# A hybrid decoder layer: the input projection as paired blocks with seven products, ahead of the three head groups

## The chip, the core and the metric

The kernel runs on one core of a Trainium2 chip. It is one program of five instruction streams, each in order: TensorE (PE; its weight loads are listed as PEld), VectorE (DVE), ScalarE (ACT), GpSimd (POOL) and SyncE (SP, which here only issues transfers). The metric is the device time of one launch in microseconds (us); the lower the better. The profile is one execution, taken by the hardware profiler.

## The reference

`x` has 1024 tokens of 1024 channels. All arithmetic is float32. One normalised input is projected onto 6144 channels, which feed three groups of heads:

```python
hn = rmsnorm(x, g_norm)
proj = hn @ w_in                      # [1024, 1024] @ [1024, 6144]
xm, zm, om, qa, ka, va, za, qx, zx = split(proj)   # 1024 x3, 512 x6
# mLSTM, 4 heads x 256
xc  = silu(causal_depthwise_conv(xm))
q_m, k_m, v_m = block_diag_proj(xc), block_diag_proj(xc), block_diag_proj(xm)
h_m = sigmoid(om) * mlstm_chunkwise(q_m, k_m / 16, v_m, *gates(q_m, k_m, v_m))
y_m = (head_layernorm(h_m) + skip * xc) * silu(zm)
# dilated attention, 8 heads x 64, three (window, dilation) patterns
y_a = dilated_attention(rope(qa), rope(ka), va) * silu(za)
# cross attention into 256 memory tokens, 4 heads x 128
kx, vx = split(rmsnorm(mem, g_mem) @ w_mem_kv)
y_x = softmax(qx @ kx.T / sqrt(128)) @ vx * silu(zx)
out = rmsnorm(x + concat(y_m, y_a, y_x) @ w_out, g_final)
```

## The kernel before

Every float32 operand of a large product is split in two parts of lower precision, `hi` and `lo`: ACT copies `hi`, DVE or POOL subtracts (`split`, L80–82). A product is then three matmuls: hi·hi, hi·lo, lo·hi. So TensorE's work is three times the plain one, and each operand costs one ACT and one DVE or POOL instruction.

The normalised input lies in SBUF for most of the run, transposed and split (`hnh`, `hnl`, eight buffers `hn` of 128 x 2 x 1024). Its weights come from DRAM in a stream of blocks, 36 channel blocks and 6 token blocks. A channel block (`ch_block`) computes 128 channels of all tokens in two halves of 512 tokens, with `proj_ch` (L161–169): 8 k-slices x 3 matmuls of 512 columns for each half. A token block (`t_block`) computes 256 channels with tokens on the partitions, in matmuls of 256 columns (L211–213). Each block has a `done` function that takes the result from PSUM: a gate `silu2` (L247–251), the rotation `rope` of queries and keys (L381–393, whose sine part needs four small transfers that swap rows), the convolution of the mLSTM (`xm_block`, L563–612), and so on. `wload` brings a block's weights, one block ahead, and splits them; a list `LO_ON_POOL` names the blocks whose `lo` POOL makes. Output blocks (`out_block`, `proj_t`, L177–179, result added by DVE at L853) stand in the same stream behind them.

The order of the work is written out in the program. The cross attention's units (head, half) come first, then the dilated attention's sixteen units, then the gates (`gates`) and the mLSTM's eight units (`head_weights`, `head_values`, `head_out`). Between the steps of a unit, `fill(n)` puts n pieces of the stream on TensorE:

```python
    for n, u in enumerate(units):
        a = head_weights(u)
        fill(HEAD_FILLS[n][0])
        if p2 is not None:
            head_out(units[n - 1], p2)
        fill(HEAD_FILLS[n][1])
        p2 = head_values(u, a)
```

So projections of x run beside the cross and the dilated attention, and output products beside the heads. On top of that a scheduler, which estimates when each operand is there, sets the final order of each engine's instructions. Results that wait for later stages (mLSTM gates `om`, `zm`, values `v`) go through DRAM; queries, keys, values and gates of the two attentions stay in SBUF, in the 13 buffers `g` of 128 x 1024. Temporaries of 128 x 512 share the four buffers `t2k`. PSUM has eight banks: `pj` 2, `s1` 3 (listed as `s`), `tp` 2, `po` 1.

## Time and profile before

| | before |
|---|---|
| timed runs, median (of 1070.48, 1071.22, 3581.81) | 1071.22 us |
| profiled execution, span | 1062.8 us |
| PE busy | 1030.0 us, 6528 matmuls |
| DVE, ACT, POOL busy | 700.4, 446.3, 309.8 us |
| moved by DMA | 117.03 MB, mean 110 GB/s |

A group's row in the profile names line, engine, operation, `output<-inputs` (buffer numbers left out), shape and count; then busy us, mean ns of one, and the engine's idle time ahead of it with what ended it. A row of busy time by stretch has the stretch, its length, busy us and instructions of each engine, the granted TensorE clock, the share of the DMA engines and GB/s. A row in order of time has start, duration, engine, line and operation; one of the chain that ended last has start, time on the chain, and what held it. A row of one line's instructions has count and shortest, median and longest duration in ns. A row of waits has the total in us, how many, and the longest.

### The profile page before, as it was taken

The page shows a single profiled execution, that of the slowest core. Times are in us where ns is not written, and L with a number is a line of the kernel's source. Part 1 is how long each engine was busy: PE and PEld are TensorE (multiplying, and loading weights), DVE is VectorE, ACT ScalarE, POOL GpSimd, SP SyncE. Part 2 cuts the span into 40 slices and gives each one's busy share as a digit, 9 for nine tenths or more (in the row PEclk, how much of TensorE's full clock was granted, in tenths as well). Part 3 has the DMA queues.
Part 4 walks back from the last instruction along what each step waited for, and adds up shares of the span by engine and source line. Part 5 has one row for each costly group of instructions (what it writes and reads, how often), then busy time and mean ns, then how long its engine had stood idle before and what let it go on. Part 6 is the DMA issues. An engine that isn't in the chain of part 4 may idle for free.

```text
span 1062.8 us, 17259 instructions
## 1 busy us (share of the span) xinstructions
PE 1030.0 (97%) x6528; PEld 920.1 (87%) x6528; DVE 700.4 (66%) x1458; ACT 446.3 (42%) x876; POOL 309.8 (29%) x296
## 2 busy tenths in 40 slices
PE   6899999999999999999999999989999999999996
PEld 4788888898889888778888888889999999999996
DVE  7865554545778578784748787735477877775375
ACT  5134433324556356563424444544344344331221
POOL 6531021408621263631000022211034144121352
PEclk8899999999999999999999999999999999999999
DMA  8333232314301131122214345344368454433332
GB/s 284 86 124 110 83 103 62 93 65 92 80 21 41 46 95 34 47 70 70 90 50 110 120 124 154 107 143 140 119 212 295 132 171 166 128 120 120 96 117 86
DMA packets 76435, 117.03 MB, mean 110 GB/s; under 512 B 14780, under 2 KB 46012, under 8 KB 76352
## 3 DMA queue, kind: packets, MB, share of 16 engines
q1 hardware_dynamic: 68032, 101.70, 29.7%
q0 software_dynamic: 8320, 14.23, 5.2%
q8 instruction: 51, 0.84, 0.3%
q14 instruction: 32, 0.26, 0.1%
HBM read 79.09 MB, written 31.57 MB: 104 GB/s over the span
## 4 chain that ended last, share of the span: by engine, by line
PE 78%; DVE 10%; DMA 6%; ACT 2%; issue 1%; POOL 1%; SPq 0%; POOLq 0%; DVEq 0%; ACTq 0%
PE pj L167 10%; PE pj L168 10%; PE pj L169 10%; PE pj L178 5%; PE pj L179 5%; PE pj L177 5%; PE pj L211 3%; PE pj L213 3%; PE pj L212 3%; PE tp L479 3%; DVE t2k L581 2%; DMA v<-P 2%; DMA wr<-in_w_out_dram 2%; PE s L454 2%; PE po L488 1%
## 5 line engine op out<-in xcount | busy, mean ns | idle before, releaser
L167 PE MATMUL pj<-hn,wh 128*128 128x512 f32 x544 | 216.8, 398 | 2.4 <-DVE t2k L249 1.3
L169 PE MATMUL pj<-hn,wl 128*128 128x512 f32 x544 | 217.0, 399 | 0.0
L168 PE MATMUL pj<-hn,wh 128*128 128x512 f32 x544 | 216.3, 398 | 0.0
L167 PEld LDWEIGHTS pj<-hn,wh 128*128 128x128 f32 x544 | 102.3, 188 | 25.6 <-DVE t2k L249 1.8
L81 ACT ACTIVATE wh<-wr 128x1024 fp32r<-128x1024 f32 x67 | 70.9, 1058 | 127.2 <-PE pj L168 53.8
L169 PEld LDWEIGHTS pj<-hn,wl 128*128 128x128 f32 x544 | 102.3, 188 | 22.7
L168 PEld LDWEIGHTS pj<-hn,wh 128*128 128x128 f32 x544 | 102.3, 188 | 22.3
L211 PE MATMUL pj<-wh,hn 128*128 128x256 f32 x384 | 107.9, 281 | 1.3 <-ACT st L262 1.3
L213 PE MATMUL pj<-wh,hn 128*128 128x256 f32 x384 | 107.5, 280 | 0.0
L212 PE MATMUL pj<-wl,hn 128*128 128x256 f32 x384 | 107.2, 279 | 0.0
L82 POOL TENSOR_TENSOR wl<-wr,wh 128x1024 fp32r<-128x1024 f32 x23 | 55.7, 2420 | 145.8 <-ACT wh L81 112.8
L82 DVE TENSOR_TENSOR wl<-wr,wh 128x1024 fp32r<-128x1024 f32 x44 | 57.0, 1296 | 46.5 <-ACT wh L81 34.9
L81 ACT ACTIVATE pth<-tp 128x512 fp32r<-128x512 f32 (+2 forms) x96 | 50.1, 540 | 73.3 <-PE tp L479 42.7
L82 DVE TENSOR_TENSOR ptl<-tp,pth 128x512 fp32r<-128x512 f32 (+2 forms) x96 | 58.0, 618 | 28.5 <-ACT pth L81 28.2
L211 PEld LDWEIGHTS pj<-wh,hn 128*128 128x128 f32 x384 | 72.1, 188 | 2.1 <-ACT st L262 1.5
L212 PEld LDWEIGHTS pj<-wl,hn 128*128 128x128 f32 x384 | 72.1, 188 | 0.4
L213 PEld LDWEIGHTS pj<-wh,hn 128*128 128x128 f32 x384 | 72.1, 188 | 0.2
L177 PE MATMUL pj<-wh,hn 128*128 128x256 f32 x256 | 71.9, 281 | 0.0
L178 PE MATMUL pj<-wl,hn 128*128 128x256 f32 x256 | 71.8, 280 | 0.0
L179 PE MATMUL pj<-wh,hn 128*128 128x256 f32 x256 | 71.7, 280 | 0.0
L462 ACT ACTIVATE P<-P,mx 128x128 f32<-128x128 f32 (+3 forms) x64 | 49.3, 772 | 21.1 <-DVE mx L458 20.8
L468 POOL TENSOR_SCALAR P<-P,ls 128x128 f32<-128x128 f32 (+4 forms) x40 | 29.2, 736 | 89.4 <-DVE ls L463 60.1
(323 smaller groups left out, 2682.4 us busy)
## 6 DMA issues: line engine op xcount, KB each, us to landing
wr<-in_w_all_dram SPq DMA_DIRECT2D x54, 512.0 KB
x<-v POOLq DMA_DIRECT2D x16, 516.0 KB, 4.5
wr<-in_w_out_dram SPq DMA_DIRECT2D x16, 512.0 KB
wr<-y SPq DMA_DIRECT2D x16, 512.0 KB
y<-t2k SPq DMA_DIRECT2D x24, 256.0 KB
v<-P SPq DMA_DIRECT2D x24, 256.0 KB
zm<-st SPq DMA_DIRECT2D x16, 256.0 KB
g<-g POOLq DMA_DIRECT2D x32, 128.0 KB, 2.7
```

The source lines that it names most:

```text
L81: S.activation(hi, src, AF.Copy)
L82: (eng_lo or V).tensor_tensor(lo, src, hi.bitcast(F32), op=SUB)
L167: PE.matmul(o, hi[:, ks], ah(k, cs), start=k == 0, stop=False)
L168: PE.matmul(o, hi[:, ks], al(k, cs), start=False, stop=False)
L169: PE.matmul(o, lo[:, ks], ah(k, cs), start=False, stop=k == KC - 1)
L177: PE.matmul(o, ah(k, cs), hi[:, ks], start=k == 0, stop=False)
L178: PE.matmul(o, ah(k, cs), lo[:, ks], start=False, stop=False)
L179: PE.matmul(o, al(k, cs), hi[:, ks], start=False, stop=k == nk - 1)
L211: PE.matmul(oi, hn_h(4 * kh + k, cs), hi[:, ks], start=kh == 0 and k == 0 and i == 0, stop=False)
L212: PE.matmul(oi, hn_h(4 * kh + k, cs), lo[:, ks], start=False, stop=False)
L213: PE.matmul(oi, hn_l(4 * kh + k, cs), hi[:, ks], start=False, stop=kh == 1 and k == 3 and i == 1)
L462: S.activation(pr, pr, AF.Exp, bias=mx, scale=-1.0, accum_out=ls)
```

## The change

The blocks of x that the start does not compute, 34 channel blocks and 6 token blocks, become 20 pairs, each computed in seven products of half the contraction length where plain block multiplication has eight. For two blocks and the two halves of the contraction, weights are `a11, a12` (first block, first and second half) and `a21, a22`; the input's quarters are `x11 .. x22` (halves of channels and of tokens). POOL makes three or four sums of weights for a pair (`unit_sums`, `unit_split`), the start makes four sums of the input (`t_build`), and DVE recombines the products from PSUM (`plus`, five additions for a pair of channel blocks, ten for a pair of token blocks).

All pairs come directly behind the start, as one stage, and all their results go to DRAM: queries with their split, rotated queries and keys, values, gates and the convolved channels `xc`. The convolution and the rotation are cut into steps in a queue `later`, of which one or two are taken behind each product. Then the mLSTM's eight units alternate with the eight of the cross attention, with only the memory's keys and values as projections. Then comes the dilated attention, whose operands `att_load` brings back from DRAM, with output products as filler, and at the end the output of that group. All weight and output splits of the stream put their `lo` on POOL. The sums of squares of x, and of the memory, are taken on TensorE by one-column matmuls against ones.

```diff
+    def t_build(k, xa, xb, t4s):
...
+        d, e = t2k(), t2k()
+        G.tensor_tensor(d, x12, x11, op=SUB)
+        G.tensor_scalar(e, x12, ga, None, op0=MUL)
+        t3, t2 = t2k(), t2k()
+        V.scalar_tensor_tensor(t3, x22, gb, e, op0=MUL, op1=SUB)
+        V.scalar_tensor_tensor(t2, x11, ga, t3, op0=MUL, op1=ADD)
...
+    def rope_done(dst, scale):
+        def done(half, o, in_sbuf):
...
+            c = t2k()
+            G.tensor_tensor(c, f, tabs["cos"][:, hs], op=MUL)
+
+            def turn():
+                G.tensor_tensor(f, sw, tabs["sin"][:, hs], op=MUL)
+                V.tensor_tensor(f, c, f, op=ADD)
+                hi, lo = st2(F32R), c.bitcast(F32R)
+                S.activation(hi, f, AF.Copy, scale=scale)
+                V.scalar_tensor_tensor(lo, f, scale, hi.bitcast(F32), op0=MUL, op1=SUB)
+                nc.sync.dma_start(dst[0][:, hs], hi.bitcast(F32))
+                nc.sync.dma_start(dst[1][:, hs], c)
+            later.append(turn)
...
+    def unit_sums(u):
...
+        G.tensor_tensor(s1_, a21, a22, op=ADD)
+        G.tensor_tensor(s2_, s1_, a11, op=SUB)
+        G.tensor_tensor(a21, a11, a21, op=SUB)
...
+    def unit_split(u, p):
+        a = sums[u][p]
+        if p == 3:
+            G.tensor_tensor(a, sums[u][2], sums[u][6], op=SUB)
...
+            split(t[:, :512], t[:, 512:], a)
...
+    def product(u, p, o, first, sub):
+        t, b = wps[u, p], side(p)
+        if units[u][0] == "c":
+            for k in range(4):
+                hi, lo = t[:, k * P:(k + 1) * P], t[:, 512 + k * P:512 + (k + 1) * P]
+                PE.matmul(o, hi, b(0, k), start=first and k == 0, stop=False, skip_group_check=True)
+                PE.matmul(o, hi, b(1, k), start=False, stop=False, skip_group_check=True)
+                PE.matmul(o, lo, b(0, k), start=False, stop=k == 3, skip_group_check=True)
...
+        if p == 1:
+            m["a"] = pj()
+            product(u, 1, m["a"], True, sub)
+            m["p1"] = tagged("ptl", [P, 512], F32, 2)
+            S.activation(m["p1"], m["a"], AF.Copy)
+        elif p == 2:
+            product(u, 2, m["a"], False, sub)
+            give(done1, 0, m["a"], False)
+        elif p == 6:
+            m["b"] = s1()
+            product(u, 6, m["b"], True, sub)
+            m["u2"] = plus(m["b"], m["p1"], tagged("pth", [P, 512], F32, 2))
+        elif p == 5:
+            m["c"] = po() if sub == 1 else s1()
+            product(u, 5, m["c"], True, sub)
+            m["u4"] = plus(m["c"], m["u2"], tagged("ptl", [P, 512], F32, 2))
+        elif p == 7:
+            product(u, 7, m["b"], True, sub)
+            give(done2, 1, plus(m["b"], m["u4"]), True)
...
+    def pairs(finish, slow):
...
+            seq += [(u, p) for p in ((1, 3, 2, 6, 5, 7, 4) if u == 0 else (1, 6, 2, 5, 7, 3, 4))]
...
+            while made < len(seq) and seq[made][0] in sums and \
+                    sum(1 if units[v][0] == "c" else 2 for v, _ in seq[n:made + 1]) <= 4:
+                unit_split(*seq[made])
+                made += 1
+            unit_step(u, p, early=u == 0)
...
+            for _ in range(2 if units[u][0] == "t" or len(later) > 12 else 1):
+                if later:
+                    later.popleft()()
...
+    for n, u in enumerate(heads):
...
+        if n + 1 < len(heads):
+            head_load(heads[n + 1])
+        a = head_weights(u)
+        if n > 0:
+            cross_values(*heads[n - 1], prev)
+            head_out(heads[n - 1], p2)
         until(f"kx{h}")
...
         prev = cross_scores(h, half)
+        until(f"vx{h // 2}")
+        if n + 1 < len(heads):
+            head_split(heads[n + 1])
+        p2 = head_values(u, a)
```

What this does to the engines' own order is shown at three places. On POOL, in the stretch of the mLSTM's input channels `xm`, before (`P` at L468 are attention weights, `wl` the weights' second part, L573 clears a buffer's edge):

```order
L468 TENSOR_SCALAR P_1097_5245<-P_1097_5245,ls_1102_5256 128x640
L573 MEMSET x_1211_5745 128x4
L573 MEMSET x_1235_5872 128x4
L82 TENSOR_TENSOR wl_5844<-wr_5841,wh_5843 128x1024
L573 MEMSET x_1259_5999 128x4
L573 MEMSET x_1283_6122 128x4
L573 MEMSET x_1306_6243 128x4
L82 TENSOR_TENSOR wl_6215<-wr_6212,wh_6214 128x1024
```

and now (L1123–1125 and L1134 are sums of weights in the raw buffers `wr` and `P`, L79 the `lo` of the convolved channels, L480 and L209 results times the norm `rsb`):

```order
L1123 TENSOR_TENSOR P_479_2913<-wr_2859 128x512
L79 TENSOR_TENSOR t2k_2796<-st_2791,t2k_2795 128x512
L209 TENSOR_TENSOR t2k_2814<-t2k_2814,rsb 128x512
L1125 TENSOR_TENSOR wr_2859<-wr_2857,wr_2859 128x512
L1124 TENSOR_TENSOR P_480_2914<-P_479_2913,wr_2857 128x512
L79 TENSOR_TENSOR t2k_2910<-st_2905,t2k_2909 128x512
L1134 TENSOR_TENSOR P_480_2914<-wr_2857,P_480_2914 128x512
L480 TENSOR_TENSOR x_475_2902<-t2k_2990,rsb 128x512
```

Where POOL had clears and a subtraction of weights now and then, sums of weights, splits and multiplications with inputs in SBUF follow one another. On DVE, in the same stretch, before (L581 are convolution steps, L577 takes the channels from `pj`, L601 adds to the gates):

```order
L581 SCALAR_TENSOR_TENSOR t2k_5807<-x_1211_5745,chv_s,t2k_5807 128x512
L584 SCALAR_TENSOR_TENSOR g_5747<-t2k_5812,t2k_5807 128x512
L581 SCALAR_TENSOR_TENSOR t2k_5876<-x_1235_5872,chv_s,t2k_5876 128x512
L82 TENSOR_TENSOR P_1227_5820<-po_5821,P_1226_5819 128x256
L601 TENSOR_TENSOR g_2014<-po_5821,g_2014 128x4x4
L82 TENSOR_TENSOR ptl_5816<-g_5747,pth_5815 128x512
```

and now (L1186 recombines a product from `s` or `pj`, L79 on `wl` and `wh` splits the weights of the coming products, L498 and L504 are the convolution):

```order
L1186 TENSOR_TENSOR t2k_2967<-s_470_2864,ptl_2934 128x512
L79 TENSOR_TENSOR wl_2975<-P_480_2914,wl_2975 128x512
L1186 TENSOR_TENSOR t2k_2990<-s_482_2921,pth_2877 128x512
L79 TENSOR_TENSOR wh_2998<-wr_2857,wh_2998 128x512
L498 SCALAR_TENSOR_TENSOR t2k_2993<-x_475_2902,chv_s,t2k_2993 128x512
L79 TENSOR_TENSOR zs_2937<-po_2944,zs_2936 128x256
L520 TENSOR_TENSOR g_2494<-po_2944,g_2494 128x4x4
```

Between two steps of the convolution now stand recombinations and splits that the next products need. On PE, in the mLSTM's heads, before (L759–761 are a head's product with the state, L177–179 output products):

```order
L177 MATMUL pj_9287<-wh_8836,hn_7886 128x256
L178 MATMUL pj_9287<-wl_8837,hn_7886 128x256
L179 MATMUL pj_9287<-wh_8836,hn_7886 128x256
L759 MATMUL tp_9350<-P_1726_8944,g_9009 128x258
L760 MATMUL tp_9350<-P_1727_8945,g_9009 128x258
L761 MATMUL tp_9350<-P_1726_8944,g_9010 128x258
L177 MATMUL pj_9319<-wh_9144,hn_9150 128x256
L178 MATMUL pj_9319<-wl_9145,hn_9150 128x256
```

and now (L643–645 project a head's queries, L722–724 are values of the unit before, L290 scores of the cross attention):

```order
L643 MATMUL pj_6739<-g_6621,wvg_6729 128x512
L722 MATMUL po_6392<-x_1032_6120,pth_6135 128x258
L723 MATMUL po_6392<-x_1033_6121,pth_6135 128x258
L724 MATMUL po_6392<-x_1032_6120,ptl_6136 128x258
L722 MATMUL po_6392<-x_1032_6120,P_1040_6150 128x258
L723 MATMUL po_6392<-x_1033_6121,P_1040_6150 128x258
L724 MATMUL po_6392<-x_1032_6120,P_1041_6151 128x258
L643 MATMUL pj_6745<-g_6621,wvg_6733 128x512
L644 MATMUL pj_6739<-g_6622,wvg_6729 128x512
L645 MATMUL pj_6739<-g_6621,wvg_6730 128x512
L290 MATMUL s_1075_6290<-hn_5156,hn_5956 128x256
L290 MATMUL s_1076_6301<-hn_5156,hn_5956 128x256
```

The runs of output products between a head's own matmuls are gone; matmuls of the next unit and of the cross attention stand there.

More of the change, by code (lines that the diff above doesn't have):

```diff
@@ L1 @@
+from collections import deque
 from contextlib import ExitStack
@@ L612, in done @@
             PE.matmul(gps2[half], wg2[:, j, :], xcl, start=False, stop=j == 7)
-        ch_block(f"xm{j}", j, done, lambda: load_wvg(j))
+            if j == 7 and half == 1:
+                gates()
+        later.extend([conv, act, values, gate])
     u_d = dram("u_d", [4, T])
@@ L983, in x_in @@
[L983 to L995 removed]
+                    PE.matmul(o, hi, hn_h(k, cs), start=n == 0, stop=False)
@@ new lines, in x_in @@
+                    PE.matmul(o, hi, hn_l(k, cs), start=False, stop=False)
+                    PE.matmul(o, lo, hn_h(k, cs), start=False, stop=n == KC - 1)
+            for c in range(2):
+                sq = tagged(("P4", "P5")[c], [P, 512])
+                S.activation(sq, x[:, c * 512:c * 512 + 512], AF.Square)
+                for i in range(4):
+                    PE.matmul(sums[:, 4 * c + i:4 * c + i + 1], sq[:, i * P:(i + 1) * P], ones,
+                              start=n == 0 and c == 0 and i == 0, stop=n == KC - 1, skip_group_check=True)
@@ new lines, in tables, with mem_load @@
+    def tables():
+        for name, src in (("cos", c_cos), ("sin", c_sin)):
+            tabs[name] = x4([P, T])
+            nc.sync.dma_start(tabs[name], src)
+            G.tensor_tensor(tabs[name], tabs[name], rsb, op=MUL)
+    def mem_load():
+        mts = late["mt"] = [x4([P, T]) for _ in range(2)]
+        for i in range(2):
+            nc.sync.dma_start(mts[i], memt[i])
+        o = tp()
+        for i in range(2):
+            for c in range(2):
+                sq = t2k()
+                S.activation(sq, mts[i][:, c * 512:c * 512 + 512], AF.Square)
+                for k in range(2):
+                    for t in range(2):
+                        first, last = (i, c, k, t) == (0, 0, 0, 0), (i, c, k) == (1, 1, 1)
+                        PE.matmul(o[:, t:t + 1], sq[:, k * 256 + t * P:k * 256 + (t + 1) * P], ones,
+                                  start=first, stop=last, skip_group_check=True)
+        late["rsmb"] = st2()[:, :256]
+        rms(o, rsm, ((0, 2, late["rsmb"]),))
```

856 lines of the change are left out of this document (481 added, 375 removed).

## The prediction

> **What bounds the kernel now.** I read the page's head first, then busy time by stretch, then the groups of instructions, then a few microseconds in order of time.
>
> ```profile
> span 1062.8 us, 17259 instructions
> PE 1030.0 (97%) x6528; PEld 920.1 (87%) x6528; DVE 700.4 (66%) x1458; ACT 446.3 (42%) x876; POOL 309.8 (29%) x296
> ```
>
> TensorE is busy for 1030.0 of 1062.8 us. The stretches below give span, then PE, PEld, DVE, ACT, POOL busy, then the granted clock, DMA share and GB/s: the start, the cross attention, the dilated attention whole and in three windows, the heads, and a window of output projection alone.
>
> ```profile
> 0.00:50.00 50.00, 37.67 (x127) 27.83 (x128) 42.44 (x38) 19.03 (x25) 31.02 (x29) 0.86 0.60 178
> 70.00:240.00 170.00, 170.00 (x1015) 149.39 (x1014) 90.67 (x206) 64.52 (x149) 32.44 (x47) 1.00 0.29 88
> 250.00:300.00 50.00, 50.00 (x245) 41.30 (x243) 33.09 (x77) 25.16 (x52) 31.00 (x34) 1.00 0.29 68
> 240.00:480.00 240.00, 236.55 (x1283) 199.47 (x1282) 177.34 (x420) 133.52 (x285) 106.39 (x112) 1.00 0.23 58
> 300.00:350.00 50.00, 49.56 (x351) 45.42 (x351) 43.19 (x119) 31.36 (x79) 9.06 (x11) 1.00 0.13 43
> 400.00:450.00 50.00, 48.40 (x252) 40.07 (x251) 40.15 (x99) 30.13 (x64) 23.89 (x24) 1.00 0.16 43
> 705.00:1012.00 307.00, 303.90 (x2459) 297.70 (x2458) 193.52 (x457) 116.59 (x223) 78.41 (x60) 1.00 0.46 152
> 950.00:1000.00 50.00, 50.00 (x427) 50.00 (x427) 23.94 (x44) 8.13 (x8) 13.01 (x6) 1.00 0.32 106
> ```
>
> After the start PE hardly stops, whichever group runs: projections fill the gaps of each. So a matmul taken away is time taken away, as long as the other engines still fit under PE. A matmul's recorded duration overlaps the next one's; its cost is the distance between starts. Column one is the start:
>
> ```profile
> 525.02 0.39 PE L168 MATMUL pj<-hn,wh 128*128 128x512 f32 x1
> ...
> 530.39 0.40 PE L167 MATMUL pj<-hn,wh 128*128 128x512 f32 x1
> 49.76 1.84 PE L236 MATMUL tp<-ones,P 128*128 128x1 f32 x16
> ```
>
> Twenty-three steps lie between the first two: 5.37/23 = 0.2335 us for 512 columns. The 427 matmuls of 950–1000 give 0.117 us for 256. One column still costs 1.84/16 = 0.115 us (the code's eight products are sixteen records).
>
> **The change, part by part.** *Products.*
>
> ```profile
> L167 PE MATMUL pj<-hn,wh 128*128 128x512 f32 x544 | 216.8, 398 | 2.4 <-DVE t2k L249 1.3 <-ACT t2k L384 1.0
> L211 PE MATMUL pj<-wh,hn 128*128 128x256 f32 x384 | 107.9, 281 | 1.3 <-ACT st L262 1.3
> ```
>
> Each line stands three times (L167–169, L211–213). Channel blocks: 3 × 544 × 0.2335 = 381 us; now 17 pairs × 7 × 12 = 1428 matmuls, 333 us. Token blocks: 3 × 384 × 0.117 = 135 us; now 3 × 336 = 1008, 118 us. Together −64.5 us, all of it on PE. The sums of squares go from 16 + 4 to 128 + 32 one-column records: 96 more in the start (11 us, under PE's 12 idle us of 0–50) and 28 more (+3 us) in the last pair. That leaves 1062.8 − 64.5 + 3 = 1001 us, were PE to stay as busy as now.
>
> *The pairs as one stage.* PE there: 451 us of products and some 34 of values, gates and weights, 485 in all. Prices for the rest:
>
> ```profile
> L427 POOL TENSOR_TENSOR t2k<-t2k,t2k 128x512 f32<-128x512 f32 x8 | 10.4, 1296 | 0.2
> L82 POOL TENSOR_TENSOR wl<-wr,wh 128x1024 fp32r<-128x1024 f32 x23 | 55.7, 2420 | 145.8 <-ACT wh L81 112.8 <-PE tp L479 12.1 <-PE s L455 8.9
> L513 POOL TENSOR_TENSOR P<-tw,bdm 128x128 f32<-128x128 f32 x32 | 18.8, 609 | 26.9 <-PE tp L236 11.0 <-DMA wvg<-P 8.2 <-DVE P L538 4.1
> L584 DVE SCALAR_TENSOR_TENSOR g<-t2k,t2k 128x512 f32<-128x512 f32 x16 | 11.1, 692 | 7.3 <-ACT t2k L583 7.2
> L82 DVE TENSOR_TENSOR wl<-wr,wh 128x1024 fp32r<-128x1024 f32 x44 | 57.0, 1296 | 46.5 <-ACT wh L81 34.9 <-issue 11.5
> L853 DVE TENSOR_TENSOR hn<-pj,hn 128x512 f32<-128x512 f32 x48 | 32.9, 686 | 32.6 <-PE pj L179 32.4
> ```
>
> POOL: 68 weight sums and differences of 512 columns, 32 multiplications of the rotation, 33 of results by the norm, 16 splits: 149 × 1.296 = 193 us; 14 of 1024 columns (12 sums, 2 tables), 34; L513's 19. Sum 246 us. DVE with two SBUF inputs: 119 splits, 28 gate ends, 32 rotation ends, 64 convolution steps, 6 query splits, 249 × 0.692 = 172 us; 21 splits of 1024, 27; gates and dilated values some 16. Sum 215 us. DVE with one input in PSUM: 114 recombinations at 0.686, 78 us, and some 43 of first results and the mLSTM's values. DVE is 336 us of 485: 69%.
>
> That would fit, but the two engines stand in each other's way:
>
> ```profile
> L812 DVE TENSOR_TENSOR t2k<-t2k,zs x16: 676/682/2875, 750.5 to 966.6; 128x512 f32<-128x512 f32 x16
> 821.45 2.68 POOL L82 TENSOR_TENSOR wl<-wr,wh 128x1024 fp32r<-128x1024 f32 x1 [0.72 <-ACT wh L81]
> 821.80 2.88 DVE L812 TENSOR_TENSOR t2k<-t2k,zs 128x512 f32<-128x512 f32 x1
> 824.60 0.68 DVE L853 TENSOR_TENSOR hn<-pj,hn 128x512 f32<-128x512 f32 x1
> 821.88 2.80 DVE t2k L812
> 824.68 0.61 DVE hn L853
> 825.33 0.50 PE pj L689
> L853 DVE TENSOR_TENSOR hn<-pj,hn x48: 668/690/692, 810.9 to 1008.3; 128x512 f32<-128x512 f32 x48
> ```
>
> L812 takes 682 ns (median), but 2875 when it begins under a POOL subtraction that runs until 824.13: it ends 0.55 us behind that. L853, one input in PSUM, never takes over 692. The three rows between are the chain that ended last: PE waits for L853, queued behind L812. The Trainium skill ("SBUF — State Buffer", *Who interferes with whom*) states it as a lock: a DVE instruction with two SBUF inputs and a GpSimd instruction that reads SBUF exclude each other, and one with at most one SBUF input is free. By that page this stage has one queue more, and these rows agree.
>
> In such a queue stand 246 + 215 = 461 us under 485 of PE. Lower bound 0: the queue fits. Upper bound: with DVE in order, its PSUM reads hide under nothing, 246 + 336 = 582, +97 us. The nearest rows lie low: 250–300 has DVE and POOL together at 64 of 50 us and PE loses nothing; 400–450 has 64 too and PE loses 1.6, which over 485 us would be 16. But in the dilated attention most DVE work reads PSUM; here it is a third. The rotations' sixteen additions also now all stand on DVE, behind POOL:
>
> ```profile
> DVE t2k L415 <- POOL t2k L392: 16.9, 6, 7.5
> ```
>
> 16.9 us of waiting in its eight additions, so up to 34 for sixteen, with all splits queued behind on DVE. I take +25 us, nearer to the rows than to the bound. PE has a cushion of about three products (8 us) by the four split buffers, less where it accumulates on a bank again.
>
> *Heads with cross attention.* By the code's counts PE has 144 matmuls of 512 columns, 48 of 384 (0.175 by proportion), 816 of about 256 and 160 of 128 (0.11): 34 + 8 + 96 + 18 = 156 us. DVE, from the two stretches that hold this work now:
>
> ```profile
> L82 DVE TENSOR_TENSOR wl<-wr,wh 128x1024 fp32r<-128x1024 f32 x12 | 16.0, 1335 | 24.8 <-ACT wh L81 13.2 <-issue 11.5
> L349 DVE TENSOR_REDUCE mx<-s 128x2 f32<-128x512 f32 x16 | 10.8, 682 | 3.4 <-PE s L347 3.4
> L82 DVE TENSOR_TENSOR ptl<-tp,pth 128x512 fp32r<-128x512 f32 x16 | 10.6, 681 | 2.9 <-ACT pth L81 2.9
> L358 DVE TENSOR_SCALAR g<-g,ls 128x256 f32<-128x256 f32 x32 | 9.2, 349 | 0.2
> L374 DVE TENSOR_TENSOR t2k<-po,g 128x512 f32<-128x512 f32 x8 | 5.5, 687 | 12.7 <-PE po L372 12.6
> ```
>
> The heads' 193.52 less output additions (L853, 32.9), weight splits (16.0 and two more) and a little of the tail is about 142; cross attention 36, its keys, values and small steps 12. That is 190 us of DVE over 156 of PE: here the order turns round, and no projection of x is left to fill in. At 100% DVE the part takes 190 us; at 43.19 of 50, the fullest attention window, 221. I take 205. Under it 18 us of attention scores and output products already stand in PE's order, and the last pair (39 us of PE, 27 of DVE) gives DVE some 9 to start earlier. PE then idles 205 − 156 − 18 − 9 = 22 us, bounds 0 and 46.
>
> *Dilated attention with the output projection.* By the code's counts PE has 97 us of attention and 135 of output products (1152 × 0.117), less those 18: 214; DVE the 177 of 240–480, less the projections' share there (some 40), plus the output additions' 33: 170 of 214 us, 79%, lighter than 300–350 (86%), where PE lost 0.44 of 50. +5 us, bounds 0 and 15. *Start and end.* Nine casts and the memory's eight steps leave DVE, 24 steps for the four sums of x and three remainders come; by the prices above that is some 18 us for 19, so DVE stays near its 42 of 50. The end keeps its instructions, with the last weights split earlier. 0, bounds −5 and +8.
>
> Sum: 1001 + 25 + 22 + 5 = 1053 us of span. The timed runs' median, 1071.22, lies 8.4 over the profiled span; with that, **1062 us**. All low bounds give about 1004, all high ones 1175.
>
> **The rivals.** *The saving arrives.* POOL runs ahead, the lock costs a few us, and DVE packs the heads: 1001 + 5 + 8 + 8.4, about 1023. For it: 250–300, and 97% PE now. Against: that had PSUM work to spread over, and projections of x as filler.
>
> *The lock decides: slower.* Each POOL operation lets one DVE one pass. If half of 246 us of POOL meets DVE's order, DVE needs 336 + 123 + 25 of waits for rotations, 484 us, as much as PE; kept from overlap by accumulations that wait on DVE, the stage pays some 80 rather than 25, and the total is 1116. It decides from 459 us of DVE, 95% of the stage. It is the page's rule at full strength; for it speaks that every lock wait in a stage without other work reaches PE, against it that L812's sixteen show only the odd long one.
>
> *Transfers.* Queries, keys, values and convolved channels now go through DRAM, and a head of the dilated attention loads 2 MB.
>
> ```profile
> wr<-in_w_all_dram SPq DMA_DIRECT2D x54, 512.0 KB
> sw<-t2k SPq DMA_DIRECT2D x64, 16.0 KB
> ```
>
> Loads, weights and sums of that part are about 36 MB; at the 152 GB/s of 705–1012 that is 237 us, over its 214. If its SP queue also waits for buffers in order, PE waits some 50 us more: 1112.
>
> **How the numbers follow.** Forecast 0.42, saving arrives 0.30, lock 0.20, transfers 0.08. Two per cent, about what can be told from no change here, is 1049.8 to 1092.6. The saving's case is faster almost whole (0.29), and of the forecast's spread (about 1040 to 1085) 0.07 is under the line; lock and transfers give 0.25 slower, a little of each staying within. So 0.36, 0.39, 0.25. The range takes in the first rival's 1023 with 10 us of start and filler, and the slower ones with 5: 1012 to 1122.
>
> **What would show it.** Right: L1158–1160 and L1167–1169 number 1428 and 1008; in the pairs' stage DVE shows two-SBUF operations of over 1.2 us that end behind POOL's, and PE between 90 and 97%; in the heads PE falls to 80–90% with DVE over 85%; in the attention PE is over 96%. Wrong: PE near 97% in the heads, or idle time in the pairs that DMA or ACT ends rather than DVE.

## The result, and the profile after

The changed kernel takes 1165.75 us (median of 1163.28 to 1167.97), the kernel before, beside it on the same chip, 1072.09: a ratio of 1.0883, with a 95% interval of 1.0852 to 1.0914. It is slower by about 94 us, and 104 us over the forecast. In the profiled execution 1164.75 us stand against a span of 1163.0, so only 1.75 us lie outside the span here.

The head of the page of the kernel after:

```profile
span 1163.0 us, 17809 instructions
PE 1041.5 (90%) x6320; PEld 918.7 (79%) x6320; DVE 861.5 (74%) x1609; ACT 507.4 (44%) x989; POOL 484.1 (42%) x388
```

PE issues 208 matmul records fewer and is yet busy for longer than before (1041.5 us against 1030.0). The view of busy time by stretch tells why; the columns are those explained ahead of the change, and the third number from the right is the granted clock:

```profile
50.00:500.00 450.00, 420.30 (x2040) 344.92 (x2039) 351.49 (x473) 171.86 (x314) 263.44 (x212) 0.98 0.42 134
500.00:550.00 50.00, 28.31 (x176) 26.89 (x177) 26.50 (x32) 18.25 (x24) 18.39 (x7) 0.73 0.17 59
650.00:850.00 200.00, 169.94 (x1106) 152.19 (x1105) 169.55 (x467) 103.66 (x249) 46.60 (x45) 0.92 0.62 194
900.00:1050.00 150.00, 147.30 (x1126) 140.57 (x1125) 109.21 (x263) 78.77 (x159) 47.29 (x38) 1.00 0.57 141
```

Where the clock is under 1.00, a matmul counts as busy for longer and does no more. So busy time flatters these stretches. I therefore priced every matmul record of the trace by its width as the prediction did (0.2335 us for 512 columns, 0.117 for 256, 0.11 for 128) and summed by stretch. The sum for the whole kernel is 963 us, 1011 before: the saving is there. What is left of a stretch is lost:

| stretch of the span, us | what runs | PE's matmuls at full price | lost | forecast |
|---|---|---|---|---|
| 0 to 50 and 1050 to 1163 | start, end | 122 of 163 | 41 | 38 (the rest of 1053 − 963) |
| 50 to 500 | the pairs | 405.5 of 450 | 44.5 | 25 |
| 500 to 550 | the pairs, gates | 21.9 of 50 | 28 | 0 |
| 550 to 850 | last pairs, heads with cross attention | 224.4 of 300 | 76 | 22 |
| 850 to 1050 | dilated attention with output products | 189.1 of 200 | 11 | 5 |

The last column is what the prediction's terms leave to each stretch; its first row is a remainder and not a term of its own. The misses are thus three: 20 us in the pairs, 28 in a hole behind them, 54 in the heads.

### The profile page after: what moved, and what is told of

It is laid out like the page before. It is cut to its first block, busy times and chain, and to the rows that moved or that the text cites. A ratio compares the mean times of both kernels' runs of the same rounds, so it can differ in the third digit from the quotient of the medians.

```text
span 1163.0 us, 17809 instructions
## 1 busy us (share of the span) xinstructions
PE 1041.5 (90%) x6320; PEld 918.7 (79%) x6320; DVE 861.5 (74%) x1609; ACT 507.4 (44%) x989; POOL 484.1 (42%) x388
## 4 chain that ended last, share of the span: by engine, by line
PE 43%; DVE 26%; DMA 12%; issue 8%; ACT 5%; POOL 4%; SPq 2%; POOLq 0%; DVEq 0%; ACTq 0%
PE pj L174 5%; PE pj L173 4%; PE pj L172 4%; DVE t2k L498 4%; PE s L1158 2%; DMA wr<-y 2%; DMA wr<-in_w_out_dram 2%; PE s L1160 2%; PE s L1159 2%; PE tp L381 2%; PE s L1168 2%; DVE wl L79 2%; PE s L1169 2%; DVE wh L79 2%; PE s L1167 2%
## 5 line engine op out<-in xcount | busy, mean ns | idle before, releaser
L172 PE MATMUL pj<-wh,hn 128*128 128x256 f32 x384 | 110.8, 289 | 4.2 <-ACT hn L78 2.2
L173 PE MATMUL pj<-wl,hn 128*128 128x256 f32 x384 | 111.8, 291 | 2.0 <-POOL wl L79 2.0
L174 PE MATMUL pj<-wh,hn 128*128 128x256 f32 x384 | 110.6, 288 | 0.0
L78 ACT ACTIVATE pth<-tp 128x512 fp32r<-128x512 f32 (+2 forms) x96 | 51.2, 540 | 75.0 <-PE tp L381 51.3
L79 POOL TENSOR_TENSOR wl<-wr,wh 128x1024 fp32r<-128x1024 f32 x20 | 47.9, 2397 | 81.8 <-ACT wh L78 79.2
L79 DVE TENSOR_TENSOR ptl<-tp,pth 128x512 fp32r<-128x512 f32 (+2 forms) x96 | 59.2, 619 | 29.3 <-ACT pth L78 28.2
L370 POOL TENSOR_SCALAR P<-P,ls 128x128 f32<-128x128 f32 (+4 forms) x40 | 25.3, 635 | 110.8 <-DVE ls L365 86.7
L79 POOL TENSOR_TENSOR hn<-wr,hn 128x1024 fp32r<-128x1024 f32 x15 | 37.2, 2489 | 58.3 <-ACT hn L78 58.3
L498 DVE SCALAR_TENSOR_TENSOR t2k<-x,chv_s,t2k 128x512 f32<-128x512 f32 x48 | 59.3, 1235 | 2.2 <-ACT t2k L496 1.9
L209 POOL TENSOR_TENSOR t2k<-t2k,rsb 128x512 f32<-128x512 f32 x21 | 36.4, 1736 | 46.1 <-DVE t2k L1186 46.1
L78 ACT ACTIVATE wh<-wr 128x512 fp32r<-128x512 f32 (+1 forms) x52 | 43.6, 839 | 23.7 <-PE s L1160 7.6
L381 PE MATMUL tp<-ident,P 128*128 128x128 f32 x288 | 49.3, 281 | 2.4 <-DVE ptl L79 2.2
L79 DVE TENSOR_TENSOR wl<-P,wl 128x512 fp32r<-128x512 f32 x47 | 46.7, 995 | 4.4 <-ACT wl L78 4.0
L79 DVE TENSOR_TENSOR wh<-P,wh 128x512 fp32r<-128x512 f32 x36 | 39.3, 1092 | 6.9 <-ACT wh L78 6.8
L381 PEld LDWEIGHTS tp<-ident,P 128*128 128x128 f32 x288 | 36.8, 145 | 6.9 <-DVE ptl L79 3.2
L1158 PE MATMUL s<-g,wl 128*128 128x512 f32 x104 | 41.7, 401 | 0.0
L1159 PE MATMUL s<-g,wl 128*128 128x512 f32 x104 | 41.0, 395 | 0.0
```

The lines of the kernel that those rows point to most:

```text
L78: S.activation(hi, src, AF.Copy)
L79: (eng_lo or V).tensor_tensor(lo, src, hi.bitcast(F32), op=SUB)
L172: PE.matmul(o, ah(k, cs), hi[:, ks], start=k == 0, stop=False)
L173: PE.matmul(o, ah(k, cs), lo[:, ks], start=False, stop=False)
L174: PE.matmul(o, al(k, cs), hi[:, ks], start=False, stop=k == nk - 1)
L209: G.tensor_tensor(t, o, r, op=MUL)
```

## The experiments

All times are medians over the rounds, and ratios are to the kernel before, run beside it on the same chip (1070 to 1072 us). Where nothing else is said, an edit is made to the kernel after, 1165.75 us.

### The pairs: which work of POOL costs what

The lock that the prediction showed at L812 is now in every stretch of the pairs. In order of time, DVE and POOL of the kernel after (start, duration, engine, line):

```profile
409.12 1.74 POOL L1123 TENSOR_TENSOR P<-wr 128x512 f32<-128x512 f32 x1
409.62 1.79 DVE L498 SCALAR_TENSOR_TENSOR t2k<-x,chv_s,t2k 128x512 f32<-128x512 f32 x1
410.82 1.75 POOL L209 TENSOR_TENSOR t2k<-t2k,rsb 128x512 f32<-128x512 f32 x1
411.33 0.68 DVE L1186 TENSOR_TENSOR pth<-s,ptl 128x512 f32<-128x512 f32 x1
411.94 1.18 DVE L498 SCALAR_TENSOR_TENSOR t2k<-x,chv_s,t2k 128x512 f32<-128x512 f32 x1
412.53 1.74 POOL L1125 TENSOR_TENSOR wr<-wr,wr 128x512 f32<-128x512 f32 x1
413.04 1.78 DVE L79 TENSOR_TENSOR wh<-P,wh 128x512 fp32r<-128x512 f32 x1
```

The first convolution step begins under a sum of weights that runs until 410.86, and ends 0.55 us behind that; the next one waits for L209 in the same way. L1186, which reads one operand from PSUM, keeps its 0.68 (0.65 to 0.69 in the whole kernel). The convolution's 48 steps serve as a gauge from here on (shortest, median, longest in ns; the row of the kernel after, then L581 of the kernel before):

```profile
L498 DVE SCALAR_TENSOR_TENSOR t2k<-x,chv_s,t2k x48: 737/1270/1786, 278.4 to 465.7; 128x512 f32<-128x512 f32 x48
...
L581 DVE SCALAR_TENSOR_TENSOR t2k<-x,chv_s,t2k x48: 734/748/2847, 554.2 to 657.5; 128x512 f32<-128x512 f32 x48
```

First the sums of weights were left out, so that the kernel's output is another:

```diff
     def unit_sums(u):
...
-        G.tensor_tensor(s1_, a21, a22, op=ADD)
-        G.tensor_tensor(s2_, s1_, a11, op=SUB)
-        G.tensor_tensor(a21, a11, a21, op=SUB)
...
     def unit_split(u, p):
-        if p == 3:
-            G.tensor_tensor(a, sums[u][2], sums[u][6], op=SUB)
```

> The sums and differences of weights on POOL are left out (three to four for each of the 20 pairs; the products take plain quarter blocks, so the output is another): some 125 us less on POOL in the pairs' stage, nothing less on DVE, ACT or TensorE. Theory (lock): DVE's two-SBUF operations wait for those; of the 45 us that TensorE loses from 50 to 500, 15 to 25 go, and some 8 more in the hole behind 500: 1133 to 1143 us; the convolution step L498 falls from a mean of 1235 ns to under 1000. Rival (DVE's own load and order, and the accumulations on a bank that wait for it): only the hole's 8 us go, 1155 to 1162, with L498 still over 1100.

It took 1119.28 us, ratio 1.0461 (1.0435 to 1.0488): 46 us less, more than either theory had, and L498 fell:

```profile
L498 DVE SCALAR_TENSOR_TENSOR t2k<-x,chv_s,t2k x48: 734/751/1794, 258.0 to 426.6; 128x512 f32<-128x512 f32 x48
```

PE loses 9 us between 50 and 450, where it lost 40. So POOL's sums cost the pairs most of what they lose. But leaving work out shortens chains too; the next two runs keep all work and only change who does it:

```diff
-            G.tensor_tensor(t, o, r, op=MUL)
+            V.tensor_tensor(t, o, r, op=MUL)
...
-            (G if in_sbuf else V).tensor_tensor(xms[j][:, 4 + x0:516 + x0], o, rsb[:, x0:x0 + 512], op=MUL)
+            V.tensor_tensor(xms[j][:, 4 + x0:516 + x0], o, rsb[:, x0:x0 + 512], op=MUL)
...
-            split(*m["x"], xct, G)
+            split(*m["x"], xct)
```

> The multiplications by the norm of results already in SBUF (L209, L480) and the split of the convolved channels, 49 operations of 512 columns, go from POOL to DVE. Lock: POOL's 49 cost the shared queue 1.3 us and more each, on DVE 0.69 each, and chains lose a hop; 1150 to 1160 us. Rival (DVE's own load): DVE gets 34 us more to do in a stage where it is 79% busy; 1175 to 1195.

1152.22 us, ratio 1.0763 (1.0746 to 1.0779): 13.5 less, as the lock has it. L498's median is at 743 ns here already, so it is a coarse gauge; its mean went from 1235 to 810, and the sums that POOL still makes are in the way of other steps (the weight splits L79 of 512 columns take 0.85 us in the mean here, 0.76 in the next run). Then the sums of weights as well (`G` to `V` in the lines of the first diff):

> Beside the 49 operations of the run before, the weight sums and differences (L1123 to L1125, L1134) go from POOL to DVE, so that POOL keeps the rotations alone in the pairs' stage and DVE gets some 66 us more. Lock theory: a POOL operation costs the shared queue at least 1.3 us, the same on DVE 0.69, so the sum of both falls; 12 to 30 us less than with the 49 alone, 1122 to 1140 us. Rival (DVE's own load counts as much): DVE then has 398 us to do in the 450 of the stage, and the gain is eaten; 1148 to 1170.

1131.93 us, ratio 1.0580 (1.0538 to 1.0622): 33.8 less than the kernel after, with the same arithmetic and *more* for DVE to do. The stretch from 50 to 450 in the kernel after, and then in this one:

```profile
50.00:450.00 400.00, 372.54 (x1811) 305.54 (x1811) 313.77 (x418) 150.74 (x276) 244.04 (x200) 0.98 0.42 133
```

```profile
50.00:450.00 400.00, 388.68 (x1907) 323.30 (x1907) 334.90 (x560) 163.45 (x294) 82.90 (x95) 0.99 0.44 140
```

Its convolution steps, as above:

```profile
L498 DVE SCALAR_TENSOR_TENSOR t2k<-x,chv_s,t2k x48: 735/742/753, 268.0 to 449.2; 128x512 f32<-128x512 f32 x48
```

DVE does 560 instructions where it did 418, for 21 us more of busy time; POOL is relieved of 161 us. What DVE's 418 had of waiting is gone, no step of L498 takes over 753 ns, and PE loses 16 us where it lost 40.

Is it the lock itself, or was POOL only a slow link in chains? On top of that kernel POOL got work whose result nobody reads:

```diff
+            if n == 56:
+                late["idle"] = tagged("P5", [P, 512])
+            if 56 <= n < 120:
+                G.tensor_tensor(late["idle"], rsb[:, :512], rsb[:, 512:], op=ADD)
```

> On the kernel with all sums and multiplications on DVE (1131.9 us), POOL adds the two halves of the norm 64 times into a buffer that nobody reads, beside the rotations and the xm pairs: 64 operations of 512 columns with SBUF inputs, some 85 us of POOL alone, no work for any other engine and no result that anyone waits for. Lock by itself: DVE's two-SBUF operations again wait, over 1.2 us in that stretch, and 15 to 45 us come back, 1147 to 1177 us. Rival (POOL cost time as a slow link in chains, not as a lock): 1129 to 1136.

1171.00 us, ratio 1.0944 (1.0923 to 1.0965): 39 us came back, from 64 operations whose results nobody waits for. The stretch in which they run, here and then without them:

```profile
240.00:340.00 100.00, 77.51 (x307) 60.05 (x306) 94.94 (x96) 27.65 (x50) 81.47 (x53) 0.92 0.26 82
```

```profile
240.00:340.00 100.00, 99.25 (x451) 81.02 (x450) 93.55 (x156) 43.66 (x79) 11.04 (x11) 1.00 0.43 136
```

DVE is shown busy for 95 and 94 of 100 us, and gets 96 instructions done in the one, 156 in the other; a weight split (L79, `wl` from `P`, 512 columns) takes it 1363 ns in the mean where it took 811. PE falls from 99 to 78 us. POOL's rotations stand behind the additions in the same queue, but DVE sat idle for them for 2.4 us only in this stretch: the time is inside DVE's own instructions. That is the lock by itself. The Trainium skill ("SBUF — State Buffer", *SBUF: two separate sides*) states it so: of a DVE operation with two SBUF inputs and a GpSimd one that reads SBUF, whichever starts first has the shared pair of ports for the whole instruction, and the other is blocked. For POOL operations with two inputs these runs agree with it. A further run asked whether the number of POOL's inputs matters:

```diff
...
+            for _ in range(3 if 56 <= n < 120 else 0):
+                if n < 84:
+                    G.tensor_scalar(late["idle"], rsb[:, :512], 2.0, None, op0=MUL)
+                else:
+                    G.memset(late["idle"], 0.0)
```

> On the kernel with all sums and multiplications on DVE (1131.9 us), POOL first multiplies half of the norm by a constant 84 times (one SBUF input), then clears a buffer 108 times (none), with no result that anyone waits for. If what stands in DVE's way is POOL's reading of SBUF, whatever the number of its inputs: DVE's operations with two SBUF inputs take over 1.0 us in the first stretch and 0.74 in the second, 1140 to 1165 us. If only POOL operations with two inputs do it: 0.74 in both, 1129 to 1136.

1151.15 us, ratio 1.0730 (1.0682 to 1.0777), the total that the lock's side named, with durations that neither did. POOL's 84 multiplications (shortest, median and longest in ns):

```profile
L1247 POOL TENSOR_SCALAR P<-rsb x84: 1488/1538/2462, 184.6 to 393.7; 128x512 f32<-128x512 f32 x84
```

L498 in groups, from 250 to 393 us under these and from 396 to 464 under the clears (count, busy us, mean ns, idle before):

```profile
L498 DVE SCALAR_TENSOR_TENSOR t2k<-x,chv_s,t2k 128x512 f32<-128x512 f32 x30 | 25.4, 847 | 0.1
...
L498 DVE SCALAR_TENSOR_TENSOR t2k<-x,chv_s,t2k 128x512 f32<-128x512 f32 x18 | 13.4, 746 | 0.1
```

An operation with one SBUF input delays DVE's steps by 0.1 us in the mean (847 against 743 ns), with POOL busy for 112 of the 150 us from 250 to 400; clears do nothing to them. In order of time, DVE's two-input steps that begin in the first 0.45 us of a multiplication take 1.04 to 1.09 us in the median, those that begin 0.6 us after its start or later 0.68. So the lock is not held for the whole of a one-input operation, and here the measurement is milder than the sentence of the Trainium skill. The run is still 19 us slower than without: DVE is at 49 of 50 us from 250 to 300, where 0.1 us for each step is time. Some 13 of the 19 are lost before the first 400 us' worth of matmuls is done; the rest is not explained.

### The hole behind the pairs

PE's waits between 500 and 550 of the kernel after, and what POOL does then:

```profile
PE tp L600 <- ACT g L594: 10.1, 1, 10.1
PE s L1167 <- ACT wh L78: 5.8, 1, 5.8
PE pj L1167 <- DVE t2k L212: 5.8, 1, 5.8
```

```profile
515.38 2.27 DVE L579 TENSOR_TENSOR_SCAN g<-x,x 4x1024 f32<-4x1024 f32 x1
521.27 1.42 DVE L593 TENSOR_TENSOR g<-x,x 4x1024 f32<-4x1024 f32 x1 [0.79 <-ACT g L588]
522.77 2.73 POOL L1123 TENSOR_TENSOR x<-P,P 128x1024 f32<-128x1024 f32 x1 [1.16 <-DVE g L593]
523.59 1.94 PE L600 MATMUL tp<-ident,g 128*128 128x128 f32 x8 [10.10 <-ACT g L594]
```

The gates (`first` to `seventh`, L560 to L601) work on rows of four partitions, one step behind the other on ACT and DVE, from about 499 to 525 us. A row of 1024 is no shorter for having four partitions: L593 takes 1.42 us, and a subtraction of 128 x 1024 took 1.30 in the kernel before (L82 in the prediction). PE waits for their transposes (L600), and POOL's sum of the next token pair's weights (L1123, into a buffer `x4`) waits for L593, since the gates' rows hold the three buffers `x4`. First I moved the two late token pairs ahead of the xm pairs, so that channel pairs, whose sums lie in other buffers, stand behind the gates:

```diff
     pair(ka_done, 28, 2)
+    pair(om_done, 16, 2, "t")
+    pair(va_done, 32, 0, "t")
     pair(xm_done, 0, 0)
...
     pair(za_done, 36, 2)
-    pair(om_done, 16, 2, "t")
-    pair(va_done, 32, 0, "t")
```

> The two last pairs of token blocks (om heads 2 and 3, va) move ahead of the xm pairs, nothing else changes. Theory (hole): the 28 us that TensorE loses between 500 and 550 us come from the gates' serial rows, whose buffers the weight sums of the next token pair wait for. With channel pairs behind the gates nothing waits for those buffers: 20 to 28 us go, about 1142 us (1136 to 1148). Rival: the serial rows stop TensorE wherever they stand, on DVE and ACT ahead of recombinations; 0 to 8 us go, 1158 to 1166.

1160.47 us, ratio 1.0842 (1.0821 to 1.0863): 5 less, the rival's figure. But the longest wait of PE had another name now:

```profile
PE tp L1280 <- ACT t2k L1276: 21.2, 1, 21.2
```

L1276 squares the memory, and the memory's load takes two buffers `x4`. It is issued at 599.1 us, just as the gates' L593 ends: the wait had gone to the next user of the same buffers. So the second try left the order of that run and took the buffers away from the question:

```diff
     def mem_load():
-        mts = late["mt"] = [x4([P, T]) for _ in range(2)]
+        mts = late["mt"] = [tagged("wr", [P, T], F32, 2) for _ in range(2)]
```

> In the order of the first run (late token pairs ahead of xm, 1160.5 us) TensorE waited 21 us for the squares of the memory, whose load took over buffers of the gates' rows. Here the memory gets two weight buffers instead. Theory (the hole is a wait for buffers that the gates' serial rows hold, and it went to their next user): 10 to 20 us less than 1160, 1140 to 1150. Rival (the rows themselves are waited for: the heads can't start before them): within 6 us, 1154 to 1165.

1142.81 us, ratio 1.0669 (1.0641 to 1.0698): 17.7 less than the order alone, 23 less than the kernel after, and the same wait is down to a quarter:

```profile
PE tp L1280 <- ACT t2k L1276: 5.6, 1, 5.6
```

The theory as put first was incomplete, since it named one waiter and not the buffer; with the buffer it holds. A try to give the gates more cover, on top of the order first tried, put three xm pairs in a row and emptied the queue of steps faster:

```diff
     pair(xm_done, 0, 2)
-    pair(zm_done, 8, 0)
     pair(xm_done, 0, 4)
-    pair(zm_done, 8, 2)
     pair(xm_done, 0, 6)
+    pair(zm_done, 8, 0)
+    pair(zm_done, 8, 2)
     pair(zm_done, 8, 4)
...
-            for _ in range(2 if units[u][0] == "t" or len(later) > 12 else 1):
+            for _ in range(2 if units[u][0] == "t" or len(later) > 4 else 1):
```

> The late token pairs go ahead of the xm pairs, three of the four xm pairs follow one another, and the queue of steps is emptied by two a product from 5 entries on, so that the gates' serial rows have some six pairs behind them in the program. Theory (the hole is a serial chain without enough work of others behind it): 10 to 20 us less than the 1160 of the order tried before, 1140 to 1150. Rival: the rows on DVE and ACT still stand between the recombinations and their products, whatever stands behind; within 5 us of it, 1155 to 1165.

1157.83 us (1149.94 to 1164.79), ratio 1.0814 (1.0751 to 1.0876), within the rival's range, though the runs spread into the theory's. In the profiled one, the slowest, the three xm pairs wait for the values' stores (`zs<-po` behind `DMA v<-zs`), and the memory's load still goes out only behind L593. Both remedies together, all multiplications and sums on DVE, the late token pairs first, and the memory in weight buffers:

> All sums and multiplications on DVE, the late token pairs ahead of xm, and the memory in weight buffers. If the lock in the pairs and the hole behind them are two separate costs: 10 to 20 us less than the 1131.9 of the first alone, 1112 to 1122 us. If the hole is the rows themselves: 1126 to 1135.

1116.58 us, ratio 1.0427 (1.0400 to 1.0455): 15.4 less than the first remedy alone. So lock and hole are two costs that nearly add: 34 and 23 us alone, 49 together. PE loses some 16 us between 50 and 500 now.

### The heads with the cross attention

Here the prediction had one price, DVE's load. Three runs take DVE's load away in three ways. In the first the cross attention does nothing but store its gate, so that the output is another:

```diff
+    def cross_left_out(h, half):
+        nc.sync.dma_start(y_d[1][half][:, h, :], xz[h][:, half * 512:half * 512 + 512])
...
-            cross_values(*heads[n - 1], prev)
+            cross_left_out(*heads[n - 1])
...
-        prev = cross_scores(h, half)
...
-    cross_values(*heads[-1], prev)
+    cross_left_out(*heads[-1])
```

> The cross attention's scores, softmax and values beside the heads are left out (the gate alone is stored in place of its result, so the output is another): about 40 us of DVE and 27 of TensorE less. Theory (DVE's load sets the heads' stage, as forecast): 35 to 45 us less, 1121 to 1131 us. Rival (each head unit is a chain in which TensorE, ACT and DVE wait in turn, and cross attention fills its holes): 5 to 20 us less, 1146 to 1161, with DVE busy under 75% of the stage and TensorE's clock still near 0.9.

1135.01 us, ratio 1.0600 (1.0578 to 1.0621): 31 us less, between the two. By the prices above it has 29 us less of matmuls, and what PE loses in the whole kernel is 202 us against 203: the gain is no more than PE's own work. Then the work stays and moves to POOL:

```diff
-            V.tensor_scalar(pr[:, i * 256:(i + 1) * 256], pr[:, i * 256:(i + 1) * 256],
+            G.tensor_scalar(pr[:, i * 256:(i + 1) * 256], pr[:, i * 256:(i + 1) * 256],
...
-            split(xs[0][:, d, :], xs[1][:, d, :], xu[:, d, :])
+            split(xs[0][:, d, :], xs[1][:, d, :], xu[:, d, :], G)
```

> In the heads' stage the 16 splits of the convolved channels and the 64 normalisations of the cross attention go from DVE to POOL: some 33 us less on DVE, some 55 more on POOL, which is 22% busy there. DVE's load sets the stage: 15 to 30 us less, 1136 to 1151 us. Rival (chains of waits, and POOL takes longer for each step): no gain, 1163 to 1180.

1161.51 us, ratio 1.0847 (1.0809 to 1.0885): 4 less, between the two. This one is no clean test: the splits have two SBUF inputs, and DVE's busy time from 655 to 850 us fell by 6 us only (160.8 against 166.7), although some 33 us of work had left it. So the third run moves work to ACT, whose copies of 512 columns (L78) take 0.62 us in the median beside the idle additions on POOL and 0.63 without them, from 240 to 340 us:

```diff
+        V.tensor_scalar(ls, ls, 0.5, None, op0=MUL)
...
-            V.tensor_scalar(pr[:, i * 256:(i + 1) * 256], pr[:, i * 256:(i + 1) * 256],
-                            ls[:, i:i + 1], 0.5, op0=MUL, op1=MUL)
+            S.activation(pr[:, i * 256:(i + 1) * 256], pr[:, i * 256:(i + 1) * 256], AF.Copy, scale=ls[:, i:i + 1])
...
-            V.tensor_scalar(gt[:, b, :], gt[:, b, :], rr[:, b:b + 1], vv[:, b:b + 1], op0=MUL, op1=ADD)
+            S.activation(gt[:, b, :], gt[:, b, :], AF.Identity, bias=vv[:, b:b + 1], scale=rr[:, b:b + 1])
```

> In the heads' stage the 64 normalisations of the cross attention and the 32 of the heads go from DVE to ACT, which takes part in no lock and is 53% busy there: some 33 us less on DVE, as many more on ACT. DVE's load sets the stage: 15 to 30 us less, 1136 to 1151 us. Rival (chains of waits through several engines set it): 0 to 8 us less, 1158 to 1166.

1165.03 us, ratio 1.0882 (1.0861 to 1.0903): nothing. The same stretch of the kernel after and of this one:

```profile
655.00:829.00 174.00, 148.20 (x952) 132.03 (x953) 150.01 (x421) 91.97 (x224) 38.96 (x40) 0.92 0.55 173
```

```profile
655.00:829.00 174.00, 148.20 (x949) 130.27 (x950) 133.09 (x372) 115.64 (x280) 38.94 (x39) 0.92 0.55 173
```

DVE goes from 150 to 133 of 174 us, and PE's 148.20 does not move by a hundredth. DVE's load does not set this stage, for all its 86%. The clock is the next candidate. This run puts matmuls that nobody reads on the same banks, ahead of the own matmuls of every unit but the first:

```diff
+        def warm(o, n):
+            for _ in range(n if u != (0, 0) else 0):
+                PE.matmul(o[:, :256], kv["kxh"][:, :P], kv["kxh"][:, :256], start=True, stop=True)
...
             o = pj()
+            warm(o, 12)
...
             o = s1()
+            warm(o, 3)
```

> In the heads' stage 36 matmuls of 256 columns whose result nobody reads go ahead of seven units' own matmuls on the same banks, 252 in all, 29 us of TensorE's time. If the lower granted clock (0.92 there) is what makes the stage long: 5 to 15 us less, 1150 to 1160 us, with the clock over 0.97. Rival (TensorE waits for the others and the clock only follows): 0 to 25 us more, 1166 to 1190.

1170.55 us, ratio 1.0938 (1.0901 to 1.0975): 4.8 more. Its busy time from 655 to 850:

```profile
655.00:850.00 195.00, 179.76 (x1311) 168.61 (x1310) 169.48 (x460) 100.81 (x240) 46.53 (x44) 0.98 0.60 189
```

The clock is 0.98 and nothing is gained by it. The Trainium skill ("TensorE: Matmul & The Clock Gate", Part 1) says that an idle window of some 3.4 us takes the clock to half; the traces fit that: behind a wait of 5.8 us in the kernel after, matmuls of 256 columns start at 506.19, 506.41 and 506.62, 0.21 us apart, where 0.117 is usual. So the low clock follows from the waits, and raising it did not shorten the stage. A gain of a few us that the added matmuls ate up again can't be told from none by this run. It says something else that is of use: 29 us of foreign matmuls cost 5 us. PE has that much room.

Next, what the units wait for by name: temporaries `t2k` (of which `ub` and `ud` hold two of four throughout a unit), and the bank `po`, which a unit's values take four times in a row:

```diff
-        ub = t2k()
+        ubd = tagged("wr", [P, 1024], F32, 2)
+        ub = ubd[:, :512]
...
-        ud = t2k().rearrange("p (a b) -> p a b", a=4)
+        ud = ubd[:, 512:].rearrange("p (a b) -> p a b", a=4)
```

> The gate rows that a head unit reads throughout (ub and ud, two of the four buffers t2k) get weight buffers that lie idle in the heads. Theory (a unit's steps queue for temporaries, so that its loads and weights start late): 8 to 20 us less than 1165.8, 1146 to 1158 us, with the hole of 600 to 655 us under 12 us. Rival (order of operations and their own latencies): 1161 to 1168.

1157.37 us, ratio 1.0796 (1.0756 to 1.0836): 8.4 less, at the edge of the theory's range. Its sign did not come, though: the stretch from 600 to 655 still loses 17 us at full price, where it lost 21 and under 12 was named.

```diff
-            o = po()
+            o = po() if b % 2 == 0 else pj()
             for s in range(b + 1):
```

> The heads' values alternate between the bank po and the two banks pj instead of taking po four times in a row. Theory (TensorE and DVE wait for one another in turn on that bank, L722 for L729 and L730): 8 to 20 us less, 1146 to 1158 us. Rival: 1161 to 1168.

1168.14 us, ratio 1.0909 (1.0871 to 1.0947): no gain. And both on the kernel of 1116.58 us:

> Both, on the kernel with all sums and multiplications on DVE, late token pairs ahead of xm and the memory in weight buffers (1116.6 us). If buffers or banks set the heads' stage: 12 to 30 us less, 1087 to 1105 us. If neither does: 1110 to 1120.

1115.20 us, ratio 1.0417 (1.0394 to 1.0439), no gain that can be told. The same with the normalisations on ACT in place of the banks:

> The kernel of 1116.6 us with the gate rows in weight buffers and the normalisations on ACT: all that may shorten the heads' stage without new work beside it. Chain theory: 1106 to 1118 us. Rival (DVE's load and buffers together): 1085 to 1105.

1118.37 us, ratio 1.0449 (1.0391 to 1.0507). The small gains don't add up. Last, the heads of the kernel *before*, with no output products between their steps:

```diff
-HEAD_FILLS = [(4, 0), (2, 2), (2, 2), (3, 1), (3, 3), (4, 3), (3, 3), (0, 2), (2, 3)]
+HEAD_FILLS = [(0, 0)] * 8 + [(2, 3)]
```

> The kernel before, with no output products between the steps of its eight head units (37 pieces of some 2.8 us, 104 us of TensorE, which then follow behind the heads). Chain theory: the units take nearly as long without them, 24 us and more each, so TensorE idles and the total rises by 30 to 70 us, 1101 to 1141 us. Rival (the heads are as long as their busiest engine: 168 us of TensorE with the om and zm projections that stay, some 110 of DVE): the products only move, 1068 to 1085 us.

1087.13 us, ratio 1.0157 (1.0119 to 1.0194): 16 us slower, just over the rival's range and far from the chain theory's. The heads' weights and values reach from 693 to 921 us there, against 692 to 952 before. Busy time of this kernel, then of the kernel before:

```profile
690.00:890.00 200.00, 182.63 (x1348) 171.39 (x1349) 132.85 (x344) 91.52 (x192) 46.50 (x46) 0.97 0.55 177
```

```profile
690.00:890.00 200.00, 195.06 (x1539) 188.74 (x1537) 124.72 (x295) 86.24 (x176) 54.21 (x46) 1.00 0.52 173
```

The units do get shorter without the products, but not as short as their PE work: PE goes from 195 to 183 of 200 us, though some 67 us of `om` projections (576 matmuls of 256 columns) still stand in the row. From 825 to 875, where hardly anything stood beside the heads, all matmuls come to 36 of 50 us at full price: 71%, about as dense as the heads of the kernel after (146 of 200, 73%).

What stays open: why the heads of the kernel after lose 54 us between 650 and 850. Neither DVE's load nor the bank sets it, a higher clock didn't shorten it, and temporaries are 8 us of it at the most. PE's waits there are many and short (the longest under 5 us, on DVE, ACT and DMA in turn), which fits a chain through several engines with nothing beside it to fill; but that no single link sets it was only seen by taking links away one at a time. Filling the stage with useful matmuls, which would be the proof, wasn't tried, since the buffers for output products are taken there. No version tried beats the kernel before: the best is 1.042 of it.

## Why the prediction was wrong

- **Products.** Right. L1158 to L1160 and L1167 to L1169 number 1428 and 1008, and PE's work by width is 963 us, where the forecast's terms give 961 (1011 less 64.5, and 14 more for the sums of squares).
- **The pairs, +25 us.** The mechanism was right, the size was not: 44.5 us lost from 50 to 500. The failed step is the choice of a value near the rows of 250–300 and 400–450 because "DVE and POOL together at 64 of 50 us" cost nothing there. In those rows DVE mostly read PSUM, which the prediction said itself and then did not price. Taking most of POOL's two-input work away is worth 34 us in the whole kernel with DVE doing it; leaving the sums out is worth 46. The sum that was called a bound, POOL's time and DVE's two-SBUF time in one queue, was the better guide. The rival "the lock decides" had 1116 us and a chance of 0.20; its mechanism held, its price of 80 us for the stage was too high, and the total was beyond it for other reasons.
- **A term that was missing.** Nothing in the sum stood for the gates' rows or for who waits on their buffers: 28 us of hole. The kernel's time fell by 15 to 23 us when the late token pairs and the memory got out of the way of the three buffers `x4`. The prediction put "gates and dilated values some 16" us of DVE down as load; as a serial chain in front of buffers it was a wait.
- **Heads with cross attention, +22 us.** This is the largest miss. The failed step is "At 100% DVE the part takes 190 us", and the 205 taken from it: DVE's load doesn't set the stage (150 to 133 us with PE's row unchanged), and the load itself was put too high, at 190 us where DVE is busy for 170 from 608 to 829. The 221 us, taken from another stage's fullest window, is what it took from 608 to 829, but that is luck, since the cause is another, and which it is stays open. The 27 us that I subtracted for work standing ahead and for an early start did not come either: the stretch from 600 to 650, in which the first unit starts, lost 19.5 us.
- **Dilated attention, +5 us.** Near enough, within its bounds of 0 and 15: 11 us lost from 850 to 1050, of which 4.4 behind 900. DMA's share is 0.87 from 850 to 900, and yet the waits of PE that a transfer ended come to 5 us in the whole kernel. So the rival of the transfers, with its 50 us, is out.
- **Start and end.** Near enough: 41 us against 38.
- **Median minus span, 8.4 us.** Wrong: 1.75 us in the profiled execution. It came from a median of runs and the span of another execution; the kernel before, too, lies 1.7 to 1.8 us over its span wherever both are of one execution.
- **What was to show it.** The signs named as right came true (two-SBUF operations over 1.2 us behind POOL's, PE at 93% in the pairs, 85% in the heads with DVE at 85%, at the edge of what was named, 98% in the attention), and the total was still off by 104 us. Their ranges were too wide to bind the sum: PE between 90 and 97% is 15 to 50 us of this stage. And busy time was the wrong gauge where the clock drops: 170 of 200 us busy in the heads are 146 at full price. One of the signs named as wrong came too, idle time in the pairs that ACT ends: in the hole it ended 16 of PE's 22 us of waits, and the hole is the term that was missing.

## What to carry to other kernels

Before work is put on POOL, add POOL's two-input SBUF operations to DVE's in the same stretch; where both are needed by the same queue of products, doing them on DVE was cheaper here even with DVE at 84% (334.9 of 400 us). One-input operations lengthened DVE's steps by 0.1 us in the mean, clears not at all. A stage that loses its independent matmuls can thin out whatever the busy shares say: the heads come to 73% of PE at full price in the kernel after, and to 71% in the kernel before where its products are taken out. And a buffer class that passes from a slow serial chain to the next stage's loads is part of that stage's critical path. Price a stage by its matmuls at full clock, not by busy time.

## What the hardware showed that was not expected

- When DVE and POOL both always have a two-input operation ready, they take turns, as in the rows at 409 to 415 us: each POOL operation (1.27 us alone, 1.74 in turn) is followed by one of DVE's (0.68 alone, 1.78 in turn).
- POOL's multiplication of 512 columns by a constant, one SBUF input, took 1.54 us, longer than a sum of two inputs (1.27 alone), and yet delayed DVE by 0.1 us in the mean, not by its length. It is not the one input that makes it slow: L370, a `tensor_scalar` of the same shape, takes 0.70 us in the kernel after, and L963, another, 2.52 at the start.
- 252 idle matmuls, 29 us of PE, cost 5 us in a stage in which PE was shown busy for 85%.
- Each `ACT_TABLE_LOAD` inside the gates' chain took 1.28 us, and the tanh of other results (L213) that came between called for another: two of them between 506 and 510 us of the kernel after.
